# Memory slabs on two sets of PSUM banks, and a query slab in four steps

## The chip, the cores and the metric

The kernel runs on one core of one Trainium2 chip. The time is device microseconds of one execution; a median is over the executions named beside it.

## The reference

Two transformer blocks of two layers each run over 512 tokens of width 1024, in float32, and both look at a memory of 256 tokens. Block one's layer is a mixer (three attentions side by side), a cross attention to the memory, and a gated feed-forward. Block two's layer is a mixer (a dilated attention with a recurrence in layer 0, a pooling in layer 1), a cross attention, and a squared-ReLU feed-forward. What the change touches is the cross attention, here block two's (block one's has no norms on queries and keys):

```python
q = rms_norm((h @ w_q).reshape(B, S, 4, 256), q_g)
k, v = jnp.split(mem_n @ w_kv, 2, axis=-1)
k = rms_norm(k.reshape(B, M, 4, 256), k_g)
v = v.reshape(B, M, 4, 256)
s = jnp.einsum('bshc,bmhc->bhsm', q, k) * (256 ** -0.5)
p = jax.nn.softmax(s, axis=-1)
o = jnp.einsum('bhsm,bmhc->bshc', p, v)
return o.reshape(B, S, D) @ w_o
```

## The kernel before

**Products.** Every float32 operand of a large product is split into a high part H and a rest L, and three matmuls (HH, HL, LH) take the place of one (`three`, L455; all go through `mm`, L223, so their line is L224). Weights come in chunks: `load_chunk` (L420) issues a DMA into a `raw` tile (a ring of 3), ScalarE writes H (L373 with a gain, L429 without), VectorE writes L (L374, L371). H and L take a slot each of the ring "w", which has 10. The same ring holds a head's keys and values for the cross attention (`kv_load`, L777: one slot for `xk`, one for `xv`).

**Slabs.** A slab is a product with 512 (or 256) columns of weights. `slab_A` (L465) has the weights' columns as output partitions, `slab_B` (L487) has tokens there: one PSUM bank a group of 128 tokens, all of them open while the chunks go by. When the last chunk is done each bank is handed to an evacuation.

**Banks.** PSUM has 8 banks in four pools: "mm" 2, "sc" 3, "tp" 2 (transposes), "ob" 1. `banks_of` (L216) names sets of them: "A" is mm, mm, tp, tp; "B" is sc, sc, sc, ob; "E" is mm, mm, sc, sc; "K" is ob, mm, mm, sc; "mm" is mm, mm. A set that is asked for with two banks takes the first two of its list.

**Memory slabs.** The memory has 256 tokens, so its slabs open two banks. `k_first` (L785, block one) makes the keys in four slabs of 256 columns, evacuated by a copy and a subtraction into `ko`. `k_second` (L795, block two) makes them in two slabs of 512 columns, evacuated by `head_norm` (L820: squares on ScalarE, L832; mean and power on GpSimd, L269 and L274; scaling on VectorE, L836) into `kn`, which is then transposed (`ktr`, L814). `mem_v` (L759) makes the values in two slabs, evacuated into `vo`. All of these slabs use the set "mm". Keys and values go to DRAM, and come back a head at a time. `k_first` runs in layer 0 behind the mixer's output product, and for layer 1 behind layer 0's feed-forward; `k_second` runs behind the feed-forward before its layer. In each of these places the output product ends with a post-norm and the next pre-norm a token tile at a time: `sqj`, `rstd`, `h` (L406, L408), a transpose `tr` (L411), and `actH`, `actL`.

**Cross attention.** `cross_heads` (L839) gives out units, one a head and a token tile. A unit's first half makes scores (`xs`, bank "sc"), their maximum (`xnm`), the exponential (L862) and the scaled `xp`; its second half transposes it (`xtr`, bank "tp"), copies it to `xpt`, and, at the fourth tile, makes the head's output (`xo`, bank of `otag`, which is "mm" in block two). `run` (L277) puts a unit's second half behind the next item's first half. The next head's keys and values are loaded at a head's first unit. Behind the second unit of a head stands a filler that makes the next head's queries. In block two (`make_q`, L1658) queries come from two slabs of 512 columns, `slab_q` (L1650): slab 0 (set "A") before the first unit, slab 1 (set "B") in the filler for head 1, each followed by head norms into `yn` and transposes `ytr` (L1668).

**Order.** Instructions go to a scheduler in the order of the program. It keeps that order as a priority, and lets an engine take a later instruction whose tiles are free and inputs ready, by times of its own. The result is a fixed order for each engine's queue.

Of the kernel before, what the change touches and what calls it, by code (L numbers as in the profile page):

```python
# [10 lines left out]
F32 = mybir.dt.float32  # L11
# [6 lines left out]
P = 128  # L18
S = 512
NT = S // P  # L20
# [134 lines left out]
def two_blocks(ctx: ExitStack, tc: tile.TileContext, I, out):  # L155
# [600 lines left out]

        return put

    def mem_v(act, wkv, vd, tag, halves=(0, 1), t_outer=False, vnew=None):  # L759
        for hf in halves:  # L760

            def ev(t, bank, hf=hf):
                for a, st in enumerate(v_out(bank)):
                    nc.sync.dma_start(out=vd[a, t, :, hf * 512:hf * 512 + 512], in_=st.bitcast(F32))

            def v_out(bank):
                if vnew is None:
                    st = r4([P, 2, 512], F32R, "vo")
                    st = st[:, 0, :], st[:, 1, :]
                else:  # L770
                    st = vnew([P, 512], F32R, "vo"), vnew([P, 512], F32R, "vo")
                put_hl(*st, bank)
                return st

            slab_B(cols_of(wkv, [(D + hf * 512, D + hf * 512 + 512)]), act, ev, tag, t_outer=t_outer)

    def kv_load(kv, h):  # L777
        kd, vd = kv
# [3 lines left out]
            "a t p n -> p (a t) n"))  # L782
        return k, v

    def k_first(act, wkv, kv, new, tag="mm"):  # L785
        kd, vd = kv
        for h in range(4):
            put = k_out(kd, h, new)

            def ev(g, bank, put=put):  # L790
                put(g, bank[:, :MEM])

            slab_A(cols_of(wkv, [(h * 256, h * 256 + 256)], nk=4), act, ev, tag)

    def k_second(act, wkv, l, kv, new, tag="mm"):  # L795
        kd, vd = kv
        gk, gq = pr(f"xak{l}"), pr(f"xaq{l}")
        g2 = sl(2, "g2")
        nc.vector.scalar_tensor_tensor(
            out=g2, in0=gk, scalar=X_SCALE, in1=gq, op0=ALU.mult, op1=ALU.mult)  # L800
        kns = [[r2([P, 512], F32, "kn") for _ in range(2)] for _ in range(2)]
        for hf in range(2):

            def ev(t, bank, hf=hf):
                head_norm(bank, kns[hf][t], 2, 256)

            slab_B(cols_of(wkv, [(hf * 512, hf * 512 + 512)]), act, ev, tag)
        for hf, kn in enumerate(kns):
            for g in range(2):
                pt = ps("tp", "ktr")  # L810
                for i in range(2):
                    gg = 2 * g + i
                    for t in range(2):
                        nc.tensor.transpose(pt[:, i * 256 + t * P:i * 256 + (t + 1) * P],  # L814
                                            kn[t][:, gg * P:(gg + 1) * P], ident)
                put = k_out(kd, 2 * hf + g, new)
                for i in range(2):
                    put(i, pt[:, i * 256:(i + 1) * 256], gain=g2[:, i:i + 1])
# [17 lines left out]
            nc.vector.tensor_scalar(dst[:, h * hd:(h + 1) * hd], bank[:, h * hd:(h + 1) * hd],  # L836
                                    r[:, h:h + 1], None, op0=ALU.mult)

    def cross_heads(make_q, q, kv, kvh, oT, otag="ob"):  # L839

        pts = {}

        def filler(h):
            make_q(h)
            yield

        def unit(h, t):
            if t == 0 and h + 1 < 4:
                kvh[h + 1] = kv_load(kv, h + 1)
            if t % 2 == 0:  # L850
                pts[h, t // 2] = [pt2([P, 2, 256], F32R, "xpt") for _ in range(2)]
            (k, v), (qh, ql) = kvh[h], q[h]
            ts = slice(t * P, (t + 1) * P)
            sc = ps("sc", "xs")
            for kk in range(2):
                three(sc[:, :MEM], k[:, kk, :], k[:, 2 + kk, :], qh[:, kk, ts], ql[:, kk, ts],
                      kk == 0, kk == 1, False)
            nm_ = sm(1, "xnm")
            nc.vector.tensor_reduce(out=nm_, in_=sc[:, :MEM], op=ALU.max, axis=AX.X, negate=True)
            p = p2([P, MEM], F32, "xp")  # L860
            ss = sm(1, "xss")
            nc.scalar.activation(p, sc[:, :MEM], AF.Exp, bias=nm_, accum_out=ss)  # L862
            rr = sm(1, "xrr")
            nc.vector.reciprocal(rr, ss)
            nc.vector.tensor_scalar(p, p, rr, None, op0=ALU.mult)
            yield
            tp = ps("tp", "xtr")
            for kk in range(2):
                nc.tensor.transpose(tp[:, kk * P:(kk + 1) * P], p[:, kk * P:(kk + 1) * P], ident)
            ph, pl = pts[h, t // 2]  # L870
            us = slice(t % 2 * P, (t % 2 + 1) * P)
            put_hl(ph[:, :, us], pl[:, :, us], tp[:, :MEM].rearrange("p (k n) -> p k n", k=2))
            if t == NT - 1:
                for m in range(2):
                    o = ps(otag, "xo")
                    ms = slice(m * P, (m + 1) * P)
                    for i in range(2):
                        ph, pl = pts[h, i]
                        for kk in range(2):
                            three(o[:, i * 256:(i + 1) * 256], v[:, kk, ms], v[:, 2 + kk, ms],  # L880
                                  ph[:, kk, :], pl[:, kk, :], kk == 0, kk == 1, True)
                    put_hl(oT.h(2 * h + m), oT.l(2 * h + m), o)

        def seq():
            make_q(0)
            for h in range(4):
                for t in range(NT):
                    yield unit(h, t)
                    if t == 1 and h + 1 < 4:
                        yield filler(h + 1)  # L890

        run(seq(), 1)


# [65 lines left out]
    def first_layer(l, act, cq, xsrc, nxt_gain, spill, mact, kv, nxt_mem, small):  # L960
# [407 lines left out]
        if kv is None:  # L1368
            kv = kv_tiles(l)
            k_first(mact, I["w_xkv"][l], kv, r4)  # L1370
        mem_v(mact, I["w_xkv"][l], kv[1], "mm")


        oT = Act(8, S, "xo")
# [73 lines left out]
    def even_layer(act, mact, kv, small):  # L1448
# [130 lines left out]
        act2, nx = next_norm("xa0")  # L1579
        wo = I["ev_w_out_2"][0]  # L1580
        out_residual([cols_of(wo, [(0, 512)]), cols_of(wo, [(512, 1024)])], mix, [2, 3, 0, 1], nx)
        mem_v(mact, I["xa_w_kv_2"][0], kv[1], "mm")
        where[0] = pt2
        return act2, mact

# [12 lines left out]
    def odd_layer(mact, kv, hs):  # L1598

        bd = a8([P, 8, _NB], F32, "band")  # L1600
        nc.sync.dma_start(out=bd, in_=I["c_band"].rearrange("p (g n) -> p g n", g=8))
        zero = pt2([P, S], F32R, "zero")
        nc.vector.tensor_scalar(zero, csb[:, :S], 0.0, None, op0=ALU.mult)
        scb = load_bcast(I["od_scale_2"][0])
        pw = a8([P, 4, 2, 256], F32, "pw")
        for g in range(4):
            nc.sync.dma_start(out=pw[:, g], in_=I["od_pool_w_2"][0, g].rearrange("(k p) n -> p k n", p=P))
            for k in range(2):
                nc.vector.scalar_tensor_tensor(
                    out=pw[:, g, k], in0=pw[:, g, k], scalar=pr("omix")[:, 2 * g + k:2 * g + k + 1],  # L1610
                    in1=scb[:, g * 256:g * 256 + 256], op0=ALU.mult, op1=ALU.mult)
        dT = [a8([P, 4, S], F32, "pd") for _ in range(2)]
        for c in range(8):
            o = ps("sc", "pb")

            mm(o, zero[:, :P], zero, True, False)
            for t in range(NT):
                n = min(_NB, S - t * P)
                mm(o[:, t * P:t * P + n], hs[t][c // 4][:, c % 4 * P:(c % 4 + 1) * P],
                   bd[:, c // 2 * 2 + min(t, 1), :n], False, t == NT - 1)  # L1620
            d = dT[c // 4][:, c % 4, :]
            if c % 2 == 0:
                nc.scalar.copy(d, o)
            else:
                nc.vector.tensor_copy(d, o)
        where[0] = p2
        mem_v(mact, I["xa_w_kv_2"][1], kv[1], "mm", (0,), vnew=pt2)
        act2, nx = next_norm("xa1")
        for t in range(NT):
            for hf in range(2):  # L1630
                o = ps("sc", "po")
                for gg in range(2):
                    for k in range(2):
                        mm(o[:, gg * 256:(gg + 1) * 256], dT[hf][:, 2 * gg + k, t * P:(t + 1) * P],
                           pw[:, 2 * hf + gg, k, :], k == 0, k == 1)
                xs = x[t][:, hf * 512:hf * 512 + 512]
                nc.vector.tensor_tensor(out=xs, in0=o, in1=xs, op=ALU.add)
            nx(t, None, None)
        mem_v(mact, I["xa_w_kv_2"][1], kv[1], "mm", (1,), vnew=pt2)
        where[0] = pt2  # L1640
        return act2

    def second_rest(l, act2, kv, mact=None):
# [6 lines left out]
        def slab_q(hf):  # L1650
# [4 lines left out]

            slab_B(cols_of(wq, [(hf * 512, hf * 512 + 512)]), act2, ev, "AB"[hf])

        def make_q(h):  # L1658
            hf = h // 2
            if h < 2:  # L1660
                slab_q(h)
            nrm = nrms[hf]
            q[h] = [r4([P, 2, S], F32R, "yq") for _ in range(2)]
            for kk in range(2):
# [3 lines left out]
                    nc.tensor.transpose(tp[:, t * P:(t + 1) * P], nrm[t][:, c:c + P], ident)  # L1668
                put_hl(q[h][0][:, kk, :], q[h][1][:, kk, :], tp)

        cross_heads(make_q, q, kv, kvh, oT, "mm")
        act3, nx = next_norm(f"mlp{l}")
        wo = I["xa_w_o_2"][l]
        out_residual([cols_of(wo, [(0, 512)]), cols_of(wo, [(512, 1024)])], oT, None, nx, "KB")
# [96 lines left out]
```

## Time and profile before

| what | before |
|---|---|
| median of 3 runs (lowest to highest) | 2866.86 us (2866.78 to 2867.74) |
| the profiled execution: time | 2867.16 us |
| its span | 2865.4 us |
| mean granted TensorE clock, of full speed | 0.998 |
| busy: TensorE, VectorE, ScalarE, GpSimd | 98%, 52%, 45%, 7% |
| mean DMA rate | 116 GB/s |

The span is the time from the first to the last instruction; the execution's time holds it. Busy time is the union of an engine's instructions. A matmul's row lasts longer than its share of the pipeline, so that TensorE's holes are read from the start of one row and the bracket of the next, which gives the idle time before it in us and what ended it. PE is TensorE, DVE VectorE, ACT ScalarE, POOL GpSimd, SP the queue that issues DMAs.

### The profile page before, as it was taken

The page shows a single profiled execution, that of the slowest core. Times are in us where ns is not written, and L with a number is a line of the kernel's source. Part 1 is how long each engine was busy: PE and PEld are TensorE (multiplying, and loading weights), DVE is VectorE, ACT ScalarE, POOL GpSimd, SP SyncE. Part 2 cuts the span into 40 slices and gives each one's busy share as a digit, 9 for nine tenths or more (in the row PEclk, how much of TensorE's full clock was granted, in tenths as well). Part 3 has the DMA queues.
Part 4 walks back from the last instruction along what each step waited for, and adds up shares of the span by engine and source line. Part 5 has one row for each costly group of instructions (what it writes and reads, how often), then busy time and mean ns, then how long its engine had stood idle before and what let it go on. Part 6 is the DMA issues. An engine that isn't in the chain of part 4 may idle for free.

```text
span 2865.4 us, 39327 instructions
## 1 busy us (share of the span) xinstructions
PE 2819.8 (98%) x14816; PEld 2376.8 (83%) x14816; DVE 1484.6 (52%) x2940; ACT 1302.0 (45%) x2656; POOL 206.8 (7%) x573
## 2 busy tenths in 40 slices
PE   8999999999999999999999999999999999999999
PEld 7868888888898778888888878888888878888887
DVE  7695554334366856543344765555334454554443
ACT  6584444333366745443333664444223344443222
POOL 2121000000011210000000210100000001000000
PEclk9999999999999999999999999999999999999999
DMA  6424633334252345333342523533332353232332
GB/s 206 130 81 138 213 111 96 98 97 131 94 171 88 89 133 184 104 103 97 99 130 95 155 68 119 167 126 97 101 96 96 119 177 110 67 110 96 96 96 74
DMA packets 235645, 333.56 MB, mean 116 GB/s; under 512 B 14656, under 2 KB 135872, under 8 KB 235456
## 3 DMA queue, kind: packets, MB, share of 16 engines
q1 hardware_dynamic: 234880, 328.96, 36.0%
q8 instruction: 116, 1.90, 0.3%
q10 hardware_dynamic: 576, 2.10, 0.2%
q14 instruction: 73, 0.60, 0.1%
HBM read 297.84 MB, written 33.16 MB: 116 GB/s over the span
## 4 chain that ended last, share of the span: by engine, by line
PE 90%; DVE 4%; ACT 4%; issue 1%; DMA 1%; POOL 1%; POOLq 0%; ACTq 0%; DVEq 0%; SPq 0%
PE pB L224 40%; PE pA L224 38%; PE xs L224 2%; PE xo L224 1%; ACT wH L373 1%; PE tr L411 1%; PE ms L224 1%; PE at L1109 1%; ACT h L380 1%; DVE wL L374 1%; PE sws L224 1%; PE mo L224 1%; PE swt L1177 1%; DVE dp L1206 1%; PE dfo L224 1%
## 5 line engine op out<-in xcount | busy, mean ns | idle before, releaser
L374 DVE SCALAR_TENSOR_TENSOR wL<-raw,par,wH 128x512 fp32r<-128x512 f32 (+2 forms) x696 | 436.9, 672 | 505.1 <-ACT wH L373 498.6
L373 ACT ACTIVATE wH<-raw,par 128x512 fp32r<-128x512 f32 (+2 forms) x696 | 417.2, 655 | 592.3 <-issue 216.4
L224 PE MATMUL pA<-actL,wH 128*128 128x512 f32 (+1 forms) x1808 | 650.1, 360 | 0.9 <-DVE actL L354 0.9
L224 PE MATMUL pA<-actH,wH 128*128 128x512 f32 (+1 forms) x1808 | 648.3, 361 | 2.6 <-ACT wH L373 1.5
L224 PE MATMUL pA<-actH,wL 128*128 128x512 f32 (+1 forms) x1808 | 648.0, 360 | 0.4 <-DVE wL L374 0.4
L224 PEld LDWEIGHTS pA<-actH,wH 128*128 128x128 f32 x1808 | 340.6, 189 | 54.8 <-ACT actH L347 1.8
L224 PEld LDWEIGHTS pA<-actH,wL 128*128 128x128 f32 x1808 | 341.5, 189 | 51.0 <-DVE wL L374 0.7
L224 PEld LDWEIGHTS pA<-actL,wH 128*128 128x128 f32 x1808 | 341.9, 189 | 50.4 <-DVE actL L354 1.5
L371 DVE TENSOR_TENSOR wL<-raw,wH 128x512 fp32r<-128x512 f32 (+1 forms) x334 | 215.2, 685 | 324.3 <-ACT wH L429 315.4
L429 ACT CAST wH<-raw 128x1024 fp32r<-128x1024 f32 (+1 forms) x168 | 175.5, 1045 | 338.6 <-PE pB L224 160.5
L224 PE MATMUL pB<-wL,mH 128*128 128x512 f32 x512 | 199.2, 389 | 0.0
L224 PE MATMUL pB<-wH,mH 128*128 128x512 f32 x512 | 198.8, 389 | 0.0
L224 PE MATMUL pB<-wH,mL 128*128 128x512 f32 x512 | 198.8, 389 | 0.0
L224 PE MATMUL pB<-wH,actH 128*128 128x512 f32 (+2 forms) x416 | 143.4, 349 | 2.2 <-ACT xp L862 1.5
L224 PE MATMUL pB<-wL,actH 128*128 128x512 f32 (+2 forms) x416 | 144.2, 347 | 0.4 <-DVE wL L374 0.4
L224 PE MATMUL pB<-wH,actL 128*128 128x512 f32 (+2 forms) x416 | 144.0, 347 | 0.0
L224 PE MATMUL pB<-wL,fH 128*128 128x512 f32 x352 | 137.5, 391 | 0.0
L224 PE MATMUL pB<-wH,fL 128*128 128x512 f32 x352 | 136.5, 390 | 0.0
L224 PE MATMUL pB<-wH,fH 128*128 128x512 f32 x352 | 136.2, 390 | 0.0
L224 PEld LDWEIGHTS pB<-wH,mH 128*128 128x128 f32 x512 | 96.1, 188 | 20.1
L224 PEld LDWEIGHTS pB<-wH,mL 128*128 128x128 f32 x512 | 96.1, 188 | 20.0
L224 PEld LDWEIGHTS pB<-wL,mH 128*128 128x128 f32 x512 | 96.1, 188 | 19.8
(361 smaller groups left out, 4666.4 us busy)
## 6 DMA issues: line engine op xcount, KB each, us to landing
raw<-in_mlp_w SPq DMA_DIRECT2D x128, 512.0 KB, 3.7
raw<-in_w_ffn_in SPq DMA_DIRECT2D x176, 256.0 KB, 3.2
raw<-in_w_ffn_out SPq DMA_DIRECT2D x44, 512.0 KB, 3.4
raw<-in_w_xkv SPq DMA_DIRECT2D x32, 512.0 KB, 4.1
raw<-in_xa_w_kv SPq DMA_DIRECT2D x32, 512.0 KB, 4.4
raw<-in_ev_w_in SPq DMA_DIRECT2D x20, 512.0 KB, 3.7
raw<-in_w_in SPq DMA_DIRECT2D x16, 512.0 KB, 4.9
raw<-in_w_out SPq DMA_DIRECT2D x16, 512.0 KB, 3.6
```

Of the source, the lines that this page charges most:

```text
L224: nc.tensor.matmul(o, a, b, start=start, stop=stop_)
L371: nc.vector.tensor_tensor(out=l, in0=src, in1=h.bitcast(F32), op=ALU.subtract)
L373: i = nc.scalar.activation(h, src, AF.Copy, scale=gain)
L374: nc.vector.scalar_tensor_tensor(out=l, in0=src, scalar=gain, in1=h.bitcast(F32), op0=ALU.mult, op1=ALU.subtract)
L380: nc.scalar.activation(junk, src, AF.Square, scale=1.0 / 32.0, accum_out=ssq[:, hf:hf + 1])
L411: nc.tensor.transpose(pt[:, i * P:(i + 1) * P], h[j][:, i * P:(i + 1) * P], ident)
L429: nc.scalar.copy(H, raw)
L1109: nc.tensor.transpose(tp[:, i * P:(i + 1) * P], src[:, i * P:(i + 1) * P], ident)
L1177: nc.tensor.transpose(tp[:, i * P:(i + 1) * P], pr[i][:, kt * P:(kt + 1) * P], ident)
L1206: nc.vector.tensor_tensor_reduce(out=pm[m], in0=sc, in1=ndt[t], scale=-DIFF_SLOPES[h], scalar=BIG, op0=ALU.add, op1=ALU.min, accum_out=nmx)
```

## The change

The memory's slabs take turns between the set "mm" and the first two banks of "B" (two "sc"): head by head in `k_first`, half by half in `k_second` and in `mem_v` when it does both halves. In block two's cross attention the second query slab is cut into four steps (`quarters`): two pairs of token tiles, each in the two banks of "mm", each in two steps of two chunks, 24 matmuls a step. The head norms of a pair follow its second step. The four chunks are kept for both pairs. A step stands behind each unit of head 0, and head 1's keys and values are loaded at the fourth unit of head 0, where they were loaded at the first.

```diff
-    def mem_v(act, wkv, vd, tag, halves=(0, 1), t_outer=False, vnew=None):
+    def mem_v(act, wkv, vd, halves=(0, 1), t_outer=False, vnew=None):
...
-            slab_B(cols_of(wkv, [(D + hf * 512, D + hf * 512 + 512)]), act, ev, tag, t_outer=t_outer)
+            slab_B(cols_of(wkv, [(D + hf * 512, D + hf * 512 + 512)]), act, ev,
+                   ("mm", "B")[hf] if len(halves) == 2 else "mm", t_outer=t_outer)
...
-    def k_first(act, wkv, kv, new, tag="mm"):
+    def k_first(act, wkv, kv, new):
...
-            slab_A(cols_of(wkv, [(h * 256, h * 256 + 256)], nk=4), act, ev, tag)
-
-    def k_second(act, wkv, l, kv, new, tag="mm"):
+            slab_A(cols_of(wkv, [(h * 256, h * 256 + 256)], nk=4), act, ev, ("mm", "B")[h % 2])
+
+    def k_second(act, wkv, l, kv, new):
...
-            slab_B(cols_of(wkv, [(hf * 512, hf * 512 + 512)]), act, ev, tag)
+            slab_B(cols_of(wkv, [(hf * 512, hf * 512 + 512)]), act, ev, ("mm", "B")[hf])
...
-    def cross_heads(make_q, q, kv, kvh, oT, otag="ob"):
+    def cross_heads(make_q, q, kv, kvh, oT, otag="ob", parts=()):
...
+        def piece(f):
+            f()
+            yield
+
         def unit(h, t):
-            if t == 0 and h + 1 < 4:
+            if t == (3 if parts and h == 0 else 0) and h + 1 < 4:
                 kvh[h + 1] = kv_load(kv, h + 1)
...
                     yield unit(h, t)
+                    if h == 0 and parts:
+                        yield piece(parts[t])
                     if t == 1 and h + 1 < 4:
                         yield filler(h + 1)
...
+        def quarters():
+
+            nrm = nrms[1] = [r2([P, S], F32, "yn") for _ in range(NT)]
+            src, n = cols_of(wq, [(512, 1024)])
+            ch, banks = {}, {}
+
+            def step(p, c):
+                if c == 0:
+                    banks[p] = banks_of("mm", 2, "pB")
+                for kc in (2 * c, 2 * c + 1):
+                    if kc not in ch:
+                        ch[kc] = src(kc, act2.gain)
+                    H, L = ch[kc]
+                    for i in range(2):
+                        ts = (2 * p + i) * P, (2 * p + i + 1) * P
+                        for k2 in range(src.nk):
+                            k = kc * src.nk + k2
+                            three(banks[p][i], H[:, k2, :], L[:, k2, :], act2.h(k, *ts),
+                                  act2.l(k, *ts), k == 0, k == act2.nk - 1, False)
+                if c == 1:
+                    for i in range(2):
+                        head_norm(banks[p][i], nrm[2 * p + i], 2, 256)
+
+            return [lambda p=p, c=c: step(p, c) for p in range(2) for c in range(2)]
+
         def make_q(h):
             hf = h // 2
-            if h < 2:
-                slab_q(h)
+            if h == 0:
+                slab_q(0)
...
-        cross_heads(make_q, q, kv, kvh, oT, "mm")
+        cross_heads(make_q, q, kv, kvh, oT, "mm", quarters())
```

The remaining lines of the diff drop the argument "mm" from the calls of `mem_v`.

## Rows read from the trace of the kernel before

**Rows 1.** The page: busy time, granted clock by slices, the chain by engine.
```profile
PE 2819.8 (98%) x14816; PEld 2376.8 (83%) x14816; DVE 1484.6 (52%) x2940; ACT 1302.0 (45%) x2656; POOL 206.8 (7%) x573
...
PEclk9999999999999999999999999999999999999999
...
PE 90%; DVE 4%; ACT 4%; issue 1%; DMA 1%; POOL 1%; POOLq 0%; ACTq 0%; DVEq 0%; SPq 0%
```
**Rows 2.** The chain that ended last: start us, us, what.
```profile
2045.14 43.52 PE pA L224 x192
```
**Rows 3.** Waits of TensorE: for whom, us in total, times, longest us.
```profile
PE tr L411 <- DVE h L406: 10.6, 3, 7.4
PE ktr L814 <- DVE kn L836: 2.7, 1, 2.7
```
**Rows 4.** Timeline of TensorE, first keys: start us, us, instruction, [idle before].
```profile
279.10 0.63 PE L411 MATMUL tr<-csb,h 128*128 128x128 f32 x4 [1.94 <-DVE h L406]
```
**Rows 5.** Timeline of VectorE at the same place.
```profile
271.59 0.68 DVE L581 TENSOR_TENSOR y<-pB,gb 128x512 f32<-128x512 f32 x1
...
278.87 0.41 DVE L371 TENSOR_TENSOR ko<-pA,ko 128x256 fp32r<-128x256 f32 x1
```
**Rows 6.** Stretches: length, busy us of PE, PEld, DVE, ACT, POOL; clock, DMA.
```profile
280.00:290.00 10.00, 10.00 (x74) 10.00 (x73) 8.56 (x18) 7.85 (x19) 1.32 (x3) 0.83 0.57 180
...
2320.00:2326.00 6.00, 5.85 (x19) 4.53 (x19) 2.39 (x5) 1.25 (x5) 0.93 (x2) 0.72 0.51 170
```
**Rows 7.** Timeline of TensorE, keys behind layer 0's feed-forward.
```profile
813.08 0.63 PE L411 MATMUL tr<-csb,h 128*128 128x128 f32 x4 [1.16 <-DVE actL L354]
814.58 0.38 PE L224 MATMUL pA<-memH,wH 128*128 128x256 f32 x1 [0.88 <-DVE ko L371]
```
**Rows 8.** Timeline of TensorE, block two's first keys.
```profile
1602.46 0.38 PE L224 MATMUL pA<-actH,wH 128*128 128x256 f32 x1 [1.52 <-ACT wH L373]
...
1604.81 0.47 PE L224 MATMUL pB<-wH,memH 128*128 128x512 f32 x1 [0.46 <-DVE kn L836]
```
**Rows 9.** Timeline of TensorE, block two's second keys.
```profile
2316.75 0.39 PE L224 MATMUL pB<-wH,memL 128*128 128x512 f32 x1
2319.86 0.33 PE L814 MATMUL ktr<-csb,kn 128*128 128x128 f32 x1 [2.72 <-DVE kn L836]
2320.34 0.47 PE L224 MATMUL pB<-wH,memH 128*128 128x512 f32 x1 [0.15 <-DVE kn L836]
```
**Rows 10.** Timelines of ScalarE and VectorE at the same place.
```profile
2317.40 0.36 ACT L832 ACTIVATE kn<-pB 128x256 f32<-128x256 f32 x1
...
2319.32 0.88 DVE L836 TENSOR_SCALAR kn<-pB,rstd_h 128x256 f32<-128x256 f32 x2 [0.99 <-POOL rstd_h L274]
2320.11 1.41 DVE L374 SCALAR_TENSOR_TENSOR wL<-raw,par,wH 128x512 fp32r<-128x512 f32 x2
```
**Rows 11.** Timeline of TensorE in block two's first cross attention.
```profile
1863.15 0.50 PE L224 MATMUL pB<-wH,actH 128*128 128x512 f32 x1 [0.76 <-ACT xp L862]
...
1871.72 1.03 PE L1668 MATMUL ytr<-csb,yn 128*128 128x128 f32 x8
...
1878.33 2.00 PE L224 MATMUL xs<-xk,yq 128*128 128x256 f32 x12
...
1887.86 0.44 PE L869 MATMUL xtr<-csb,xp 128*128 128x128 f32 x2 [0.81 <-DVE xpt L371]
```
**Rows 12.** Stretches of block two's cross attentions, first and second layer.
```profile
1860.00:1870.00 10.00, 9.24 (x46) 7.59 (x45) 2.46 (x8) 2.46 (x7) 0.00 (x0) 1.00 0.00 0
1878.00:1888.00 10.00, 8.11 (x58) 6.96 (x57) 9.42 (x29) 6.81 (x22) 2.09 (x5) 1.00 0.33 111
2415.00:2425.00 10.00, 9.24 (x46) 7.61 (x45) 2.20 (x8) 2.21 (x7) 0.00 (x0) 1.00 0.00 0
2433.00:2443.00 10.00, 8.21 (x59) 7.00 (x57) 9.43 (x30) 7.06 (x23) 2.34 (x5) 1.00 0.34 119
```
**Rows 13.** Loads of a head's keys in that cross attention: issue to landing.
```profile
DMA to landing us min/median/max: 4.3/5.2/7.1
```

More of the change, by code (lines that the diff above doesn't have):

```diff
@@ L1370, in first_layer @@
             k_first(mact, I["w_xkv"][l], kv, r4)
-        mem_v(mact, I["w_xkv"][l], kv[1], "mm")
+        mem_v(mact, I["w_xkv"][l], kv[1])
         oT = Act(8, S, "xo")
@@ L1581, in even_layer @@
         out_residual([cols_of(wo, [(0, 512)]), cols_of(wo, [(512, 1024)])], mix, [2, 3, 0, 1], nx)
-        mem_v(mact, I["xa_w_kv_2"][0], kv[1], "mm")
+        mem_v(mact, I["xa_w_kv_2"][0], kv[1])
         where[0] = pt2
@@ L1626, in odd_layer @@
         where[0] = p2
-        mem_v(mact, I["xa_w_kv_2"][1], kv[1], "mm", (0,), vnew=pt2)
+        mem_v(mact, I["xa_w_kv_2"][1], kv[1], (0,), vnew=pt2)
         act2, nx = next_norm("xa1")
@@ L1638, in odd_layer @@
             nx(t, None, None)
-        mem_v(mact, I["xa_w_kv_2"][1], kv[1], "mm", (1,), vnew=pt2)
+        mem_v(mact, I["xa_w_kv_2"][1], kv[1], (1,), vnew=pt2)
         where[0] = pt2
```

## Prediction

> **What bounds the kernel now.** I read the page first. TensorE is busy 2819.8 of 2865.4 us and carries 90% of the chain that ended last; VectorE and ScalarE carry 4% each [rows 1]. In the long feed-forward stretches it runs without a hole: 192 matmuls of 512 columns in 43.52 us, 0.2267 us each [rows 2]. Work cannot be taken from it by this change, which removes and adds no instruction; only TensorE's holes can shrink. So I went to the list of its waits, where the largest entries are transposes behind the scaled rows of a normalization and key transposes behind `kn` [rows 3], and then to its timeline around each memory slab. The reader is to see there the same picture four times: a key slab ends, the next one needs the same two "mm" banks, and these are still being emptied, while the normalization that would feed the transposes is not ready either. The granted clock, a row of full speed on the page [rows 1], has two dents, right behind two of these holes. Last I took busy time by stretches of block two's cross attention.
>
> **The key and value slabs, place by place.**
>
> Block one, layer 0, keys. Slab 0 ends and TensorE stands 1.94 us until four transposes whose `h` comes late [rows 4]; slab 1 cannot fill this, because slab 0's banks are emptied only from 278.87 on, behind the normalization's work in VectorE's queue [rows 5]. With the "sc" banks slab 1 starts at once: their last reader was the third tile's evacuation at 271.59 [rows 5] (the fourth tile lies in "ob"). The granted clock of 280 to 290 us is 0.83 [rows 6]: 10 x 0.17 = 1.7 us lost at the lower level of 1.2 GHz, with TensorE busy throughout that window and idle shortly before. If the hole goes I expect the dent to go with it. Gain 1.94 + 1.7 = 3.6 us; at least 0 (slab 1's weights late), at most 3.6.
>
> Block one, behind layer 0's feed-forward. Holes of 1.16 and 0.88 us, the second one literally on `ko`, slab 0's evacuation [rows 7]. The clock is not touched here. Gain 2.0, bounds 0 and 2.0.
>
> Block two, first keys (`k_second`). Holes of 1.52 and 0.46 us; in the first TensorE had even gone on to the next stage's slab and waited for its weights, in the second it waits for `kn` [rows 8]. Slab 1 in "sc" fills both: gain 2.0, bounds 0 and 2.0.
>
> Block two, second keys. Here the whole chain of a head norm is exposed: slab 0 ends at 2317.14, and the next matmuls start at 2319.86 and 2320.34, holes of 2.72 and 0.15 us [rows 9]. The chain is two squares on ScalarE from 2317.40, a power on GpSimd, and the scaling on VectorE from 2319.32, 0.88 us [rows 10]. Slab 1's weights are no obstacle: the last of its four chunks is being split from 2320.11 on, 1.41 us [rows 10], so it is there at 2321.5, and it is needed three chunks of 12 matmuls later than 2317.14, 3 x 12 x 0.2267 = 8.2 us, at 2325.3. The dent costs 6 x 0.28 = 1.7 us [rows 6]. Together 2.72 + 0.15 + 1.7 = 4.6. What is late next: the first value slab, whose first chunk is split on ScalarE behind slab 1's own squares. That order I cannot see; I take off half of one chunk's split, 0.7, and count 3.9. Bounds 0 and 4.6.
>
> The value slabs of block one and of block two's first layer alternate as well; the trace has no hole of note between them, so I count nothing. Where one half is done alone (block two's second layer) the tag stays "mm".
>
> Sum of the slabs: 3.6 + 2.0 + 2.0 + 3.9 = 11.5 us. A hole that is filled early counts in full only if TensorE has work behind it: after each there are further key matmuls, a value slab or a query slab. Below nothing a place would go only if the next stage's "sc" tiles waited for slab 1's evacuation; before, its "mm" tiles waited for that same evacuation, so I set no loss.
>
> Here a rule speaks against the change. The Trainium skill, page "TensorE: Matmul & The Clock Gate", section "HAM oscillation — how this bites in real kernels", tells of a thin matmul whose clock fell in its waits, and says: "Adding PSUM double-buffering gave no further gain". By it the slabs would give nothing and the sum would be the steps alone. Its waits were for weights from DMA; here the timeline names the evacuation of a bank (`ko`, `kn`) in three places of four, so I follow the rows and keep the rule as a rival.
>
> **The query slab in four steps.** Before, block two's second query slab is a block of 96 matmuls (96 x 0.2267 = 21.8 us) in "sc", "sc", "sc", "ob", between the second and the third unit of head 0. Its banks and the units' scores fight for "sc": the slab waits 0.76 us for a unit's exponential [rows 11], 1860 to 1870 is busy only 9.24 of 10. When it is over, the units that were held back, four head norms and the splits of the next weights fall on VectorE together: 9.42 of 10 us, and TensorE drops to 8.11; the second layer repeats it with 9.24 and 8.21 [rows 12]. The holes are 0.76 + 1.89 = 2.65 and 0.76 + 1.79 = 2.55 us. The largest single one, 0.81, waits for VectorE's part of a unit [rows 11].
>
> After, two token tiles at a time go through "mm", in steps of 24 matmuls, 5.4 us, each between two units. That hides a unit's softmax behind 5.4 us of matmuls, and two of the four head norms move to the middle. Four things are added, in order:
> - Step 1 needs "mm", which the first query slab fills with its first two tiles. These are done first and normalized while the other two run; no wait.
> - Step 3 opens "mm" again behind the head norms of step 2. The chain from squares to scaled rows is 2317.40 to 2320.20 = 2.8 us [rows 10], the first bank starts it half a chunk, 6 x 0.2267 = 1.4 us, before the step's end: 1.4 us exposed for one bank. TensorE has the eight query transposes of head 1, 1.03 us, and scores of units 2 and 3, twelve matmuls in 2.0 us [rows 11], which need only "sc": covered. Without this cover it costs 1.4 to 2.8.
> - The output of head 0 (`xo`, otag "mm") stands behind the head norms of step 4: again 1.4 us, and TensorE's queue behind it has head 1's units, if their keys are there.
> - Head 1's keys and values: the four chunks take 8 of the 10 slots of the weight ring, head 0's keys two, so this load is moved from before the first unit to the fourth, and its slots come free only with step 3. A load lands 4.3 to 7.1 us after its issue, median 5.2 [rows 13]. Step 4 is 5.4 us and unit 3 lies beside it: just covered at the median, 1.7 us late at the maximum. On SP only output weights stand behind it, needed much later.
>
> I take off 1.1 us a layer, most of one bare bank wait of 1.4: 2.6 - 1.1 = 1.5, 3.0 us for two layers. Bounds a layer: +2.6 (all holes go) and, with both bank waits bare (2 x 2.8) and the load 1.7 late, 2.6 - 7.3 = -4.7.
>
> **The sum.** 11.5 + 3.0 = 14.5 us. The profiled execution took 2867.2 us with a span of 2865.4, 0.3 above the median of the three runs, 2866.9; the 1.8 us around the span stay. 2867.2 - 14.5 = 2852.7, from the median 2852.4. **Forecast 2852.5 us.**
>
> **Rivals.**
> - Only the slabs pay. The steps' new waits eat what the old holes cost: 2867 - 11.5 = 2855.5, or 2860 when a part of the slab gain goes too. For it: VectorE at 9.42 of 10 [rows 12] is a load that no new order takes away. Against: it is 10 us long, and stretches beside it have room.
> - The holes come back. Key slabs run earlier, so weights and normalizations are met earlier and TensorE waits for these instead: of 11.5 us only the two clock dents (3.4) or less remain, 2861 to 2867. For it: one hole of the four is already a wait for weights [rows 8]. Against: at 2317 the weights were ready in time [rows 10]. By the Trainium skill's rule above, slabs at zero and steps at 3.0, it is 2864.
> - Slower: the weight ring. With eight slots held by the steps, head 1's keys can be issued only when step 3 is through. With both bank waits bare TensorE stands 2.8 us before step 3 and 2.8 before `xo`, and two holes of that size each bring a dent of 1.7 as at 277 and 2317. The load adds 1.7 if it is issued with step 3's end, and all of its 7.1 if SP has it behind an output-weight load that waits for a slot of step 4. So 10.7 to 16.1 a layer, less the 2.6 that go: 8.1 to 13.5, two layers 16 to 27, and with the slabs' 11.5 a time of 2872 to 2883, 2877 in the middle. It decides once the new holes pass 2.6 + 5.8 = 8.4 us a layer. Against it: the scores and transposes that are free to run there.
>
> **How the numbers follow.** A measurement of this kernel tells 0.2%, 5.7 us, from no change: faster is below 2861, slower above 2872.6. Forecast 0.50, only the slabs 0.22: both faster, 0.72. The holes come back 0.16, the same. The ring 0.12, counted as slower. The low end is all holes and dents filled: 3.6 + 2.0 + 2.0 + 4.6 + 5.2 = 17.4 us, so 2850, plus what a smoother unit stage may give in holes too small for the rows here; I allow 8 us for that, 2842. The high end takes in most of the third case: 2865. The forecast's own range is 2846 to 2858.
>
> **What would show it.** Right: in the new trace no wait on `h`, `ko` or `kn` of over 1 us behind the first key slabs; no dent of the clock behind them; the busy share of the stretch after the query slab near 9.5 of 10, VectorE's below 9. Wrong: a wait of TensorE for weights where these holes were; a hole before step 3 or before head 0's `xo` of over 2 us; the scores of head 1 waiting for `xk`.

## The result, and the profile after

The changed kernel took **2846.5 us** (median of four executions, 2844.7 to 2846.6) against 2867.3 of the kernel before beside it: a ratio of 0.9926, 95% interval 0.9909 to 0.9943. The forecast was 2852.5 us: the direction was right, and where a gain of 14.5 us was forecast 20.8 were measured.

The page of the changed kernel (busy us, the granted clock by slices, the chain by engine), which answers to [rows 1]:

```profile
PE 2811.9 (99%) x14816; PEld 2373.4 (83%) x14816; DVE 1484.0 (52%) x2940; ACT 1300.6 (46%) x2656; POOL 208.5 (7%) x573
...
PEclk9999999999999999999999999999999999999999
...
PE 93%; DVE 3%; ACT 3%; issue 1%; POOL 0%; DMA 0%; POOLq 0%; ACTq 0%; DVEq 0%; SPq 0%
```

Nothing was added or removed; TensorE's part of the chain rises from 90% to 93%, VectorE's and ScalarE's fall by one each. The list of TensorE's waits (us in total, times, longest):

```profile
PE tr L411 <- DVE h L406: 8.6, 2, 7.3
...
PE pb L224 <- DVE zero L1610: 0.5, 1, 0.5
PE xo L224 <- DVE yn L837: 0.5, 2, 0.3
```

Of [rows 3] the wait of 2.7 us on `kn` is gone, and `tr` on `h` has lost one time and 2.0 us; what is left of it lies at the start of the execution. Stretches of 20 to 26 us over the four key stages, answering to [rows 4 to 9] (columns as in [rows 6]):

```profile
276.00:296.00 20.00, 20.00 (x169) 19.97 (x169) 18.50 (x38) 16.72 (x41) 4.62 (x8) 1.00 0.78 239
801.00:827.00 26.00, 26.00 (x221) 26.00 (x220) 23.82 (x51) 22.39 (x54) 3.90 (x8) 1.00 0.81 256
1580.00:1605.00 25.00, 25.00 (x124) 20.82 (x123) 23.37 (x39) 22.29 (x52) 9.04 (x17) 1.00 0.62 185
2293.00:2315.00 22.00, 22.00 (x100) 18.20 (x99) 15.22 (x25) 14.58 (x32) 3.11 (x8) 1.00 0.69 222
```

and the first two of them in the kernel before:

```profile
276.00:296.00 20.00, 18.06 (x140) 17.89 (x140) 16.99 (x34) 15.72 (x37) 3.77 (x8) 0.91 0.65 199
801.00:827.00 26.00, 23.82 (x182) 22.44 (x182) 23.50 (x50) 22.50 (x57) 6.01 (x13) 1.00 0.68 215
```

TensorE is busy in each microsecond of the four, at full clock, and starts 169 matmuls where it started 140. Its timeline shows how: the groups of four transposes of `h` now stand among the slabs' matmuls, each when its `h` is there (these two and two between them), where [rows 4] had the first behind a hole.

```profile
281.93 0.60 PE L411 MATMUL tr<-csb,h 128*128 128x128 f32 x4
...
292.11 0.60 PE L411 MATMUL tr<-csb,h 128*128 128x128 f32 x4
```

Block two's first and second cross attention, answering to [rows 12]:

```profile
1856.00:1866.00 10.00, 10.00 (x51) 8.31 (x50) 2.61 (x9) 2.87 (x9) 0.00 (x0) 1.00 0.31 101
1866.00:1876.00 10.00, 9.56 (x72) 8.49 (x70) 8.78 (x23) 7.29 (x24) 2.02 (x4) 1.00 0.83 269
...
2415.00:2425.00 10.00, 9.38 (x66) 8.00 (x64) 9.91 (x27) 7.31 (x21) 1.43 (x3) 1.00 0.73 238
```

and TensorE's timeline in the first of them, answering to [rows 11]:

```profile
1867.44 0.88 PE L224 MATMUL xs<-xk,yq 128*128 128x256 f32 x6
...
1869.87 0.98 PE L224 MATMUL xo<-xpt,xv 128*128 128x256 f32 x6 [0.27 <-DVE yn L837]
...
1876.19 0.50 PE L224 MATMUL pB<-wH,yoL 128*128 128x512 f32 x1 [0.32 <-DVE yoL L371]
```

The stretch with the steps has no hole; behind it the largest is 0.32 us, where it was 0.81. `xo` waits 0.27 us for head norms.

**Where the 20.7 us came from.** Both traces hold 14816 matmuls, stage by stage the same number, so the start of the n-th one in each can be subtracted at every stage's end:

| stage | forecast | gain, us |
|---|---|---|
| start of the execution | 0 | 0.3 |
| first keys of block one | 3.6 | 3.6 |
| from there to block one's first scores | 0 | 0.75 |
| keys behind layer 0's feed-forward | 2.0 | 2.9 |
| layer 1's value slabs | 0 | 0.9 |
| block two, first keys | 2.0 | 2.45 |
| block two, second keys | 3.9 | 5.1 |
| block two, two cross attentions | 2 x 1.5 | 2 x 2.4 |

Together 20.7 us before rounding, the difference of the two profiled executions (2867.16 and 2846.49 us). The slabs have 15.7 of it, the steps 4.8. The 0.3 us at the start are chance: other profiled executions differ by more there.

### The profile page after: what moved, and what is told of

Same layout as the page of the kernel before. It is cut to its first block, busy times and chain, and to the rows that moved or that the text cites. A ratio compares the mean times of both kernels' runs of the same rounds, so it can differ in the third digit from the quotient of the medians.

```text
span 2844.7 us, 39320 instructions
## 1 busy us (share of the span) xinstructions
PE 2811.9 (99%) x14816; PEld 2373.4 (83%) x14816; DVE 1484.0 (52%) x2940; ACT 1300.6 (46%) x2656; POOL 208.5 (7%) x573
## 4 chain that ended last, share of the span: by engine, by line
PE 93%; DVE 3%; ACT 3%; issue 1%; POOL 0%; DMA 0%; POOLq 0%; ACTq 0%; DVEq 0%; SPq 0%
PE pB L224 42%; PE pA L224 39%; PE xs L224 2%; PE xo L224 1%; PE tr L411 1%; PE ms L224 1%; PE at L1116 1%; PE sws L224 1%; PE mo L224 1%; PE swt L1184 1%; DVE dp L1213 1%; ACT wH L373 1%; PE dfo L224 1%; PE swo L224 1%; PE po L224 0%
```

## The experiments

"The planner" in the expectations is the scheduler that fixes each engine's order. Medians of the kernel before beside these runs were 2865.8 to 2867.0 us.

**Slabs alone.** The kernel before with only these lines of the change (in `mem_v` where both halves are done):

```diff
-            slab_A(..., act, ev, tag)
+            slab_A(..., act, ev, ("mm", "B")[h % 2])
...
-            slab_B(..., act, ev, tag)
+            slab_B(..., act, ev, ("mm", "B")[hf])
```

> The kernel before with the slabs of keys and values alternating between the two sets of banks; block two's second query slab stays one block. Theory (the two parts of the change fill separate holes, and their gains add): the stages of the slabs gain as in the changed kernel, keys of layer 0 3.6 us, the stretch behind them to the first scores 0.75, keys behind layer 0's feed-forward 2.9, value slabs and mixer output of layer 1 0.9, block two's first keys 2.45, its second keys 5.1, together 15.7 us: 2867.3 - 15.7 = 2851.6 us, ratio 0.9945, both clock dents at 280 and 2321 us gone, nothing gained in block two's cross attention. Rival (the parts need one another: an earlier end of the slabs only feeds the stages that the steps smooth): less than 12 us or more than 18, and block two's cross attention moves as well.

Measured 2851.6 us, ratio 0.9948 (0.9936 to 0.9960). Its stages gain 3.6, 0.75, 2.8, 0.9, 2.45 and 5.1, as in the changed kernel, and its cross attentions in block two nothing.

**Steps alone.** The changed kernel with every memory slab in "mm":

```diff
-                   ("mm", "B")[hf] if len(halves) == 2 else "mm", t_outer=t_outer)
+                   "mm", t_outer=t_outer)
```

(and the same in `k_first` and `k_second`).

> The changed kernel with all key and value slabs back in the one set of banks that they had before; only the query slab in four steps is left of the change. Theory (gains add): 2.4 us in each of the two cross attentions of block two and nothing elsewhere, 4.8 in all: 2862.5 us, ratio 0.9983; holes and dents at 280 and 2321 us are there as before. Rival 1 (the steps gain only because the slabs before them end earlier): below 1 us, 2866 to 2867. Rival 2 (the steps carry more than their own stage): over 7 us, below 2860.

Measured 2862.3 us, ratio 0.9982 (0.9973 to 0.9991); 2.4 us in each cross attention; elsewhere its trace gains 0.4 us behind the keys at 812 and loses 0.7 behind the second keys of block two. The product of the two ratios is 0.9930: the parts add up, and neither rival holds.

**Value slabs alone.**

```diff
-            slab_B(cols_of(wkv, ...), act, ev, tag, t_outer=t_outer)
+            slab_B(cols_of(wkv, ...), act, ev, ("mm", "B")[hf] if len(halves) == 2 else "mm", ...)
```

> The kernel before with only the two value slabs alternating; keys and query slab as before. The prediction counted nothing for these, the comparison of the two traces shows 0.75 us between layer 0's query slab and its first scores and 0.86 us in layer 1's value slabs. Theory (both come from the value slabs' banks): those two stages gain 0.75 and 0.86, all key stages nothing, 1.6 in all: about 2865.7 us. Rival (the first of them comes from the keys being done earlier): 0.86 or less, and the first scores of layer 0 wait some 0.5 us for the query as before.

One execution, 2866.4 us. The stages named gain 0.75 and 0.86 us. Block one's first scores waited before for both parts of the query, copied out behind a split of weights; TensorE and ScalarE there, kernel before:

```profile
333.56 0.62 PE L224 MATMUL xs<-xk,xq 128*128 128x256 f32 x3 [0.48 <-ACT xq L373]
```
```profile
331.32 1.71 ACT L373 ACTIVATE wH<-raw,par 128x256 fp32r<-128x256 f32 x4 [7.76 <-PE pA L224]
332.94 1.06 ACT L373 ACTIVATE xq<-pA 128x512 fp32r<-128x512 f32 x2
```

With the value slabs on two sets that wait is gone:

```profile
332.49 1.12 PE L224 MATMUL xs<-xk,xq 128*128 128x256 f32 x8
```

So the 1.6 us that I had counted as nothing are the value slabs' own; by what path their banks bring the query earlier was not followed. Its key stages did not repeat the kernel before, though no line of them differs: the dent at 280 us was missing, and one stood at 814. That led to the last experiment.

**A useless product in the hole.** The kernel before, in `k_second` of layer 1 behind the first slab:

```diff
+            if l == 1 and hf == 0:
+                jk = ps("sc", "jk")
+                for j in range(26):
+                    mm(jk[:, :MEM], act.h(j % 4, 0, P), act.h(4 + j % 4), j == 0, j == 25)
```

> The kernel before with 26 useless matmuls of 256 columns (products of the memory's tiles that nobody reads, into a free bank) put behind the first key slab of block two's second keys, where TensorE stands 2.72 us and then runs 3.4 us at half the clock. By the 0.11 us that one takes they fill 2.9 us, just the hole. Theory (the dent is the hole's consequence and costs 1.7 us): the granted clock stays full there, the next slab starts at the same time as before and ends 1.5 to 1.7 us earlier, so about 2865.5 us in all. Rival (the dent is owed to something else there, or the half clock costs nothing because the matmuls wait for weights or columns anyway): the dent stays or goes with a gain of less than 0.5 us, 2867.

One execution, 2867.9 us: no gain. The hole is full and there is no dent. Against [rows 6] its stretch behind the hole has 28 matmuls started for 19, at full clock:

```profile
2320.00:2326.00 6.00, 5.99 (x28) 4.82 (x28) 2.40 (x5) 0.32 (x2) 1.59 (x2) 1.00 0.47 161
```

By the starts of the matmuls TensorE is 1.6 us ahead of the kernel before at 2326, but the time is given back at once. TensorE, ScalarE and VectorE at the end of the second slab:

```profile
2333.89 0.47 PE L224 MATMUL pB<-wH,memH 128*128 128x512 f32 x1 [1.62 <-ACT wH L373]
```
```profile
2327.00 4.06 ACT L373 ACTIVATE wH<-raw,par 128x512 fp32r<-128x512 f32 x6 [6.68 <-PE pB L224]
2330.96 0.36 ACT L836 ACTIVATE kn<-pB 128x256 f32<-128x256 f32 x1
```
```profile
2332.87 0.87 DVE L840 TENSOR_SCALAR kn<-pB,rstd_h 128x256 f32<-128x256 f32 x2 [0.97 <-POOL rstd_h L274]
```

A new hole of 1.62 us stands ahead of the value slab. The profile names a weight split, but the value slab's four chunks are two splits each, and by 2331.06 eight are done; what ended 0.15 us before the matmul, at 2333.74, is the scaling of `kn`, which empties the bank that the value slab shares with the second key slab. In this kernel the scheduler put six splits ahead of the squares of `kn` on ScalarE. In the kernel before the first token tile's squares stand ahead of these splits:

```profile
2327.75 0.39 ACT L832 ACTIVATE kn<-pB 128x256 f32<-128x256 f32 x1 [6.49 <-PE pB L224]
```

There no hole stands ahead of the value slab, in any of the three looks below. So the new hole comes from the shared banks and from this order together, and what a filled hole is worth in the old order is not shown. The theory fell in its sum. That the filling took the dent away is not shown either: two of those three looks have no dent here with the hole open.

**The four steps in one block.** The changed kernel, its steps all in the filler for head 1:

```diff
+            if h == 1:
+                for f in quarters():
+                    f()
...
-        cross_heads(make_q, q, kv, kvh, oT, "mm", quarters())
+        cross_heads(make_q, q, kv, kvh, oT, "mm")
```

> The changed kernel, but block two's four query steps run one behind the other in the old place, between the second and the third unit of head 0 (head 1's keys are loaded early again, as before). So the query slab still uses the mm banks and no longer takes the units' sc banks, only the taking turns with units is gone. Theory (the turns carry the gain: a unit's softmax and the head norms are hidden by matmuls of the steps between): 2.4 us a layer are lost again, and the third step waits bare for the head norms of the second, up to 2.8 us a layer: 2846.5 + 4.8 = 2851 us, up to 2857, holes in block two's cross attention only. Rival (it is enough that slab and scores no longer fight for the sc banks): 2846.5 to 2848 us.

Measured 2862.1 us, ratio 0.9979 (0.9970 to 0.9988): 15.6 us over the changed kernel, where the theory allowed 10.5. The rival is out: leaving "sc" for "mm" is not enough. Timeline of TensorE, a stretch behind its first large wait, and its waits:

```profile
1867.33 0.44 PE L1703 MATMUL ytr<-csb,yn 128*128 128x128 f32 x2 [2.10 <-DVE yn L837]
1867.81 0.47 PE L224 MATMUL pB<-wH,actH 128*128 128x512 f32 x1
...
1882.13 0.44 PE L1703 MATMUL ytr<-csb,yn 128*128 128x128 f32 x2 [1.33 <-DVE yn L837]
```
```profile
1866.00:1874.00 8.00, 6.63 (x22) 5.18 (x23) 1.75 (x4) 0.42 (x3) 1.58 (x3) 0.79 0.02 9
```
```profile
PE ytr L1703 <- DVE yn L837: 7.2, 5, 2.1
```

These are the prediction's bare bank waits, in the place that its slower rival gave them (two transposes of `yn` slip in ahead; the third step itself opens at 1867.81, 0.14 us after the scaling that empties its bank), with a dent behind (8 x 0.21 = 1.7 us; its trace has three in the two layers). It is the taking turns with the units that hides them.

**Head 1's transposes earlier.**

```diff
-                    if t == 1 and h + 1 < 4:
+                    if t == (0 if parts and h == 0 else 1) and h + 1 < 4:
```

> The changed kernel with head 1's eight query transposes asked for one unit earlier, ahead of the second step, so that they are not left to lie between the second and the third. The prediction said that the third step's wait for its banks is covered by these transposes and two units' scores and costs 1.4 to 2.8 us a layer without that cover. Theory: a hole of 0.5 to 1.8 us before the third step (the scores still cover a part), 2847.5 to 2850 us. Rival (the planner finds other work, or the wait was shorter than the chain of rows suggested): no hole over 0.3 us there, 2846.5 us.

Measured 2846.1 us, ratio 0.9929 (0.9915 to 0.9943), no different from the changed kernel; in the trace 0.5 us a layer faster. Its timeline, from head 1's first scores on:

```profile
1867.63 1.94 PE L224 MATMUL xs<-xk,yq 128*128 128x256 f32 x15
...
1870.51 1.90 PE L224 MATMUL xo<-xpt,xv 128*128 128x256 f32 x14
```

No hole stands ahead of the third step, and `xo` waits for no norm. The cover that the prediction saw in these transposes isn't needed: the units' scores do it. The theory fell.

**The head outputs in "ob".**

```diff
-        cross_heads(make_q, q, kv, kvh, oT, "mm", quarters())
+        cross_heads(make_q, q, kv, kvh, oT, "ob", quarters())
```

> The changed kernel with the head outputs xo of block two back in the ob bank, which the query slab in steps no longer uses. Theory (head 0's xo waits 0.27 us for the head norms of step 4 only because it shares mm with them): this wait goes, 0.3 to 0.5 us a layer, 2845.5 to 2846 us, too little for the timing and to be seen in the trace only. Rival (ob is one bank against mm's two and is also the first bank of the output projection, so a second xo waits for the first's evacuation): 1 to 2 us a layer slower, 2848 to 2850 us.

Measured 2852.5 us, ratio 0.9952 (0.9938 to 0.9965): the rival is right in sign and too low in size, 3 us a layer. Stage by stage, 1.6 to 1.8 us a layer are lost in the cross attention and as much behind it, up to the feed-forward. Its waits:

```profile
PE tr L411 <- DVE actL L354: 2.4, 3, 0.8
...
PE pB L224 <- ACT yoH L370: 1.8, 4, 0.7
```

In the changed kernel the wait of `xo` is 0.27, and the first of these is 0.8 in all. That fits the rival's reason, a bank that looks free and is the output projection's first; the rows name the head outputs' evacuation (`yoH`), not the bank, so the reason is argued.

**Two early moves.** In block two all heads' transposes behind the first unit, and the pooling stage's tile of zeros made a stage earlier:

```diff
-                    if t == 1 and h + 1 < 4:
+                    if t == (0 if parts else 1) and h + 1 < 4:
...
-        zero = pt2([P, S], F32R, "zero")
-        nc.vector.tensor_scalar(zero, csb[:, :S], 0.0, None, op0=ALU.mult)
```

(the last two lines now stand in `pool_in`).

> The changed kernel with two small moves: in block two every next head's query transposes are asked for one unit earlier (behind the first unit of the head before it), and the tile of zeros that the pooling stage starts with is made one stage earlier. Theory (the waits of 0.26 to 0.32 us on the query tiles in heads 2 and 3, and the 0.52 us on the zero tile, are there only because these are asked for late): 0.5 us a layer for head 1, up to 0.9 for heads 2 and 3, and 0.5 for the zeros: 1.5 to 3.3 us in all, 2843 to 2845 us. Rival (the transposes then displace scores and the first output projection from where they filled holes; an early tile of zeros takes a buffer from the keys' halves): 2846 to 2849 us.

Measured 2844.1 us, ratio 0.9924 (0.9911 to 0.9938). The trace has 0.5 us a layer and 1.0 at the pooling; for heads 2 and 3 the move gains nothing, since other waits take the place of the old ones:

```profile
1879.76 0.98 PE L224 MATMUL xs<-xk,yq 128*128 128x256 f32 x6 [0.54 <-ACT xp L867]
1883.27 0.98 PE L224 MATMUL xs<-xk,yq 128*128 128x256 f32 x6 [0.44 <-ACT yq L370]
```

Then both were timed on one chip, unchanged:

> The changed kernel once more, timed beside the kernel with the two early moves. Theory: 2846.5 us, and no dent of the clock behind any key slab, since there is no hole: its times lie closer together than those of the kernel before. Rival (the dents come by chance even without a hole of note): one behind a key slab in this look, times spread over 5 us as before.

> The changed kernel with the query transposes of every next head one unit earlier and the tile of zeros one stage earlier, timed beside the changed kernel on one chip. Theory: 2.0 us faster than that (0.5 a layer and 1.0 at the pooling stage, as the traces showed), 2844.3 us. Rival (the difference of the first timings was the chip's or the start's): within 0.7 us of it.

The changed kernel took 2846.3 us (2844.8 to 2847.4), ratio 0.9931 (0.9919 to 0.9944), with no dent behind a key slab and a spread of 2.5 us, where nine executions of the kernel before beside it spread over 5.7; the one with the early moves 2844.6 (2843.3 to 2845.0). Over both times its ten executions lie between 2843.3 and 2845.1, the changed kernel's nine between 2844.7 and 2847.4: some 2 us faster than the changed kernel, below what the ratios to the kernel before can tell, and by the traces the sum of stages that moved.

**The kernel before, unchanged.**

> The kernel before, unchanged, profiled once more. Theory (the dent of the clock is a matter of chance once there is a hole; in four profiled executions with the same holes it stood at 280 us in three and at 814 us in one): holes of the same size at 277, 812, 1601 and 2317 us, but not the same dents; 0 to 3 of them, the one at 2321 the likeliest. Rival (the dents follow from the program; the other place was due to that kernel's edit): dents at 280 and 2321 us exactly as in the first profile.

> The kernel before, unchanged, profiled a third time. Theory and rival as for the second look: by the theory the same holes with another set of dents is likely in one of the two looks, and the time of an execution goes with their number, 1.7 us each; by the rival all three profiles show the same two.

2866.7 and 2864.0 us. The holes of the second look, and three stretches around them:

```profile
279.70 0.63 PE L411 MATMUL tr<-csb,h 128*128 128x128 f32 x4 [1.93 <-DVE h L406]
...
812.18 0.63 PE L411 MATMUL tr<-csb,h 128*128 128x128 f32 x4 [1.15 <-DVE actL L354]
813.68 0.39 PE L224 MATMUL pA<-memH,wH 128*128 128x256 f32 x1 [0.88 <-DVE ko L371]
...
2320.22 0.33 PE L814 MATMUL ktr<-csb,kn 128*128 128x128 f32 x1 [2.54 <-DVE kn L836]
```
```profile
278.00:288.00 10.00, 8.30 (x70) 8.33 (x71) 9.87 (x22) 9.61 (x25) 3.12 (x7) 1.00 0.71 220
810.00:818.00 8.00, 5.97 (x36) 5.53 (x36) 8.00 (x19) 7.26 (x20) 2.27 (x5) 0.79 0.76 236
2317.00:2326.00 9.00, 6.31 (x28) 4.79 (x27) 4.49 (x8) 3.63 (x12) 2.22 (x4) 1.00 0.56 189
```

and of the third, where all that these rows show comes 2.5 to 4 us earlier than in the first:

```profile
276.60 0.41 PE L411 MATMUL tr<-csb,h 128*128 128x128 f32 x2 [1.93 <-DVE h L406]
...
2317.25 0.33 PE L814 MATMUL ktr<-csb,kn 128*128 128x128 f32 x1 [2.69 <-DVE kn L836]
```
```profile
278.00:288.00 10.00, 10.00 (x87) 10.00 (x86) 9.61 (x21) 8.29 (x19) 1.31 (x3) 1.00 0.74 219
810.00:818.00 8.00, 7.39 (x49) 7.39 (x50) 7.50 (x19) 5.96 (x17) 1.50 (x3) 0.79 0.87 271
2317.00:2326.00 9.00, 8.60 (x39) 7.02 (x40) 3.82 (x9) 3.52 (x13) 2.08 (x4) 1.00 0.39 120
```

The holes are those of [rows 4, 7, 9], to 0.2 us. The dents are not: 280 and 2321 us in the first look, 814 in the second, 811 in the third. The rival is out.

Nor is a dent that stays away all gain. By the starts of the matmuls the full clock behind the second keys saves 1.6 us in the second and the third look, but 20 us later only 0.6 to 0.8 are left, because the pooling stage then waits longer for its tile of zeros (first, second, third look):

```profile
2346.38 0.50 PE L224 MATMUL pb<-zero 128*128 128x512 f32 x1 [0.55 <-DVE zero L1603]
```
```profile
2345.97 0.50 PE L224 MATMUL pb<-zero 128*128 128x512 f32 x1 [1.38 <-DVE zero L1603]
```
```profile
2343.18 0.50 PE L224 MATMUL pb<-zero 128*128 128x512 f32 x1 [1.58 <-DVE zero L1603]
```

In the changed kernel this wait stays at 0.5.

## Why the prediction came out as it did

- **The bound.** That only TensorE's holes could shrink, and that the slabs' holes are bank waits: right. The slabs alone give what the table says. I counted two dents of the granted clock in that trace; there is a third, at 68.5 us, and the changed kernel has one there too, at 68.0. The rule that I had kept as a rival gives nothing for a second set of banks; here it gave 15.4 us by itself, so for this kernel the measurement decides against it. The Trainium skill's page ("TensorE: Matmul & The Clock Gate", section "HAM oscillation — how this bites in real kernels") tells it of one thin matmul, after its loop had been reordered; to hold it against waits on an evacuation was my reading.
- **First keys of block one**, 3.6: as forecast in this pair of executions, but by luck. By the starts of the matmuls the hole gave 2.1 us and the dent 1.5, where I had 1.94 and 1.7; and I took the dent for the hole's sure consequence. Of six profiled executions with these key slabs (three looks at the kernel before, the steps alone, the value slabs alone, the useless product) three lack it, and the place is then worth 2.1 us. But each of the six has exactly one dent at the two places of block one, 280 or 811 to 814: one dent for both together was a fair term, its place was not.
- **Keys behind layer 0's feed-forward, and block two's first keys**, 2.0 each: measured 2.9 and 2.45. I summed the idle brackets. A hole costs more, from start to start: in [rows 9] the matmuls of 2316.75 and 2319.86 are 3.11 us apart where 0.23 would do, 2.88 us for a bracket of 2.72. With that the holes of [rows 7] are 1.3 and 1.0, and a third of 0.3 us that I had left out goes too.
- **Block two's second keys**, 3.9: measured 5.1: the upper bound of 4.6, the 0.16 that the bracket leaves out, and some 0.3 that lie in no wait. The 0.7 us taken off for weights that come late was wrong: no such wait appears. It rests on a misreading. Counted from the first of the 16 loads of keys and values, the last chunk of slab 1 is the eighth, which ScalarE splits from 2316.16 on; what VectorE splits at 2320.11 [rows 10] is the value slab's first chunk, ready before slab 1 had done a quarter of its matmuls.

```profile
2316.16 1.33 ACT L373 ACTIVATE wH<-raw,par 128x512 fp32r<-128x512 f32 x2 [1.64 <-DMA raw<-in_xa_w_kv]
```

- **Value slabs**, nothing: measured 1.6. "No hole of note" was the step that failed: the 0.48 us ahead of block one's first scores stood in the trace, and in layer 1 two restarts of 0.4 and 0.2 us, too short for a bracket.
- **Steps**, 1.5 a layer: measured 2.4. Of the 1.1 us taken off for bare bank waits 0.27 came true, at `xo`, where I had put it. Step 3 had no wait. The load of head 1's keys was issued at 1861.35 and landed 4.0 us later, as these rows of its queue and of the DMAs show, 2.1 us ahead of head 1's first scores at 1867.44; the forecast had it just covered.

```profile
1861.35 0.37 SPq L781 DMA_DIRECT2D xk<-kd  x1
```
```profile
xk<-kd SPq DMA_DIRECT2D x1, 512.0 KB, 4.0
```

- **What would show it.** No wait on `h`, `ko` or `kn` over 1 us, no dent, 9.56 and 9.38 of 10 behind the query slab: right. VectorE below 9 there: right in the first layer (8.78), wrong in the second (9.91), where TensorE is busy 9.38 us for 9.56.
- **The rivals.** Only the slabs pay: out, the steps give 4.8 by themselves. The holes come back: out in the changed kernel, though one came back behind the useless product. The slower one needed both bank waits bare; the block of four steps makes them so, and then loses 10.5 us against the slabs alone (2862.1 and 2851.6).

The sum missed 6.2 us: 0.3 at the start, 2.5 on the keys, 1.6 on the values, 1.8 on the steps. All have the same sign: each doubt was taken off a term, while small holes and restarts were left out. So the sum for all holes and dents filled, 17.4 us, was passed, as the allowance of 8 us for small holes had left open, and the result lies at the low end of the forecast's own range of 2846 to 2858.

## What to carry to other kernels

Where one stage's slabs follow each other through the same PSUM banks, the evacuation of each is a hole of the next; another set of banks removes it; the one try to fill a hole with other work gained nothing here. Price a hole from start to start of the matmuls around it, not by its bracket, and count the small ones. Cut a block of matmuls into pieces that reuse one pair of banks only where other work takes turns with them: the same pieces in a row were slower than the block they replaced.

## What was not expected of the hardware

A hole of the same length brings a dent of the clock in one execution and none in the next, with the same program. Three looks at the kernel before, with the same holes, had dents behind its key slabs at 280 and 2321, at 814, and at 811 us. Holes of 2.54 and 2.69 us at 2317 left the clock at full (2.4 GHz) in two of them, and those of 1.15 and 0.88 were followed by the lower level of 1.2 GHz for a while (0.79 of full speed over 8 us: 1.7 us by that figure, 1.5 by the starts of the matmuls). The times go with it: of the 15 executions of the kernel before that were timed beside the slabs alone, those with a mean granted clock of 0.999 took 2864.1 to 2866.1 us, those with 0.998 2865.6 to 2868.8, the one with 0.997 2870.9. The third look, the fastest of the three, also lacks a dent at 68 to 70 us that every other profiled execution has. What decides whether a hole is followed by a dent stays open. For a forecast it means that the place of a dent read from one profile is a chance, and that several profiles are needed for its price: of the five executions with the hole at 2317 open, three had the dent behind it.
